# Five kinds of stores issued from GpSimd's queue instead of SP's, in a one-core decoder step

## The chip, the cores and the metric

The kernel runs on one core of one Trainium2 chip. The metric is the device time of one execution in microseconds (us), the median of several runs; lower is better. Engines are named as in the profile: PE (TensorE: matmuls, with its weight loads as PEld), DVE (VectorE), ACT (ScalarE), POOL (GpSimd) and SP (SyncE, which computes nothing here and only issues DMAs). A DMA can be issued from the instruction stream of SP, ACT or POOL. An engine works through its stream in order: a DMA that must wait for its data holds up whatever stands behind it in the same stream.

## The reference

One layer of a hybrid decoder for a prompt of 1024 tokens and 8 sample tokens that share all weights. With d = 1024:

```python
sc_b, sc_c, sc_x, z, xbc, dt_raw, q, gates = jnp.split(xn @ w_in, splits, axis=-1)
conv_u = causal_conv(sc_c * sc_x, width 3)
y_a = (sc_b * conv_u) @ w_sc_out                       # branch A: gated short convolution
...
y_ssd, ssm_new = ssd_fn(xs, dt, a, bm, cm, ssm_s0)     # branch B: 32 heads x 64, state 128
y_ssd = (y_ssd + ssm_d * xs) * silu(z)
y_b = group_rmsnorm(y_ssd, ssm_norm_w, 4) @ w_ssm_out
...
y_c = softmax(q @ mem_k) @ mem_v @ w_attn_o            # branch C: 4 heads x 256, 256 memory tokens
merged = g_a * y_a + g_b * y_b + g_c * y_c             # g = sigmoid(gates)
x = x + merged @ w_merge_o
x = x + swiglu(rmsnorm(x))                             # hidden size 2816
```

The prompt's scan runs in 8 chunks of 128 tokens. Each sample token has its own recurrent state (8 samples x 32 heads x 64 x 128), which is updated once: s = s * exp(dt * a) + (dt * x) * B, and y = s . C. The updated states are outputs, too.

## The kernel before

The kernel is written with a tile framework: it writes instructions in program order, and the framework orders them on the engines, places tiles in a fixed number of buffers per tag, and inserts the semaphore waits. Prompt and sample tokens stand side by side as 1032 columns. Every float32 matmul is done as three: weights and activations are split into a high part (ACT copy) and a rest (DVE subtraction), lines 152 and 153. Raw weights are loaded by SP into a tag with three buffers (line 53, load_raw at line 121), so a raw load has to wait until the DVE has read the raw block three loads earlier.

The stages that the diff touches:

- **Scan stage** (about 540 to 1300 us of the span). PE works on projections of w_in as filler: first the short convolution (sc_step, lines 603 to 634: three projections for each of 8 column blocks, and at the end of the third the DVE's multiplication at line 631 and the store of the result to the scratch array sc_d), then the queries, then the gates. Within each gemm, at three marks, one piece of the scan of branch B is put in (tick, line 168). The scan goes over 4 groups of 8 heads (lines 1173 to 1191), one after another, and for each group over 8 chunks. A chunk c has three pieces (lines 901 to 931): p1 (transposes of x into xp, the products bp/cbm, xdt on the DVE, xdd on POOL; the load r of the decay rows for chunk c + 2, a broadcast of ac_d; s_read for sample c - 2), p2 (matmul pss of chunk c - 1, the state's sum on the DVE, POOL's decay of the state, s_step for sample c - 1, ACT's exponentials of r for chunk c + 1, s_load for sample c + 1) and p3 (matmuls po and py, output yt). r, st and raw weights have three buffers each.
- **Sample states**, inside those pieces: s_load (line 866) loads a state block st of 128 partitions x 512 elements, s_step (line 873) updates it on POOL with lines 879 and 882, and s_read (line 884) stores it to the output and reads it out on the DVE. Of the group's pieces p1 of chunk c holds s_read(c - 2), a round after s_step.
- **End of a group**: z_pieces multiply by silu(z), and group_norm (line 973) ends with four multiplications on the DVE (line 980), each followed by a store of its tile xg[t] to yb_d. The x tiles of the next group are loaded (line 1183) into buffers of the same tags, the third and fourth of them into buffers which these stores read.
- **Attention and output stage** (about 1300 to 1690 us). Filler on PE: the output projections (out_part, line 1420). For every block m a gate tile gt is loaded, multiplied with the matmul's result, added to an earlier partial sum from mg_d in the second and third round, and stored to mg_d. out_in (line 1413) loads the activations of a round. In the pieces run the prompt's attention and, on the side, the samples': s_scores loads key blocks kc into two buffers, s_out (line 1291) does eight samples, and for each stores four rows of 256 elements to os_d; s_back (line 1310) reads os_d back.

Before the change SP issues nearly all loads and these stores; ACT issues stores of its own results (queries, gates, convolved x, attention outputs). POOL issues no DMA at all. In the scan stage POOL runs xdd (776), decay (828), the two lines of s_step and small copies and memsets; in the attention and output stage it runs nothing.

Of the kernel before, what the change touches and what calls it, by code (L numbers as in the profile page):

```python
# [21 lines left out]
TT = T + NS  # L22
# [19 lines left out]
def tile_kernel(ctx: ExitStack, tc, a, o):  # L42
    nc = tc.nc
    V, S, G, PE, SY = nc.vector, nc.scalar, nc.gpsimd, nc.tensor, nc.sync
# [4 lines left out]
    def bc(ap, shape):  # L49
        return ap.to_broadcast(shape)  # L50
# [13 lines left out]
    def sm_ps(name):  # L64
        return psm.tile([P, 512], F32, tag="sm", name=name)

    def dram(name, shape):
        return dp.tile(shape, F32, tag=name, name=name)
# [4 lines left out]
    def flat(ps):  # L73
        return ps[:, :, :CW]

    def t3(t, lo=0):
        return t[:, lo : lo + TT].rearrange("p (n c) -> p n c", n=NCH)
# [78 lines left out]
    def ev_tile(name, shape=(P, TT + 4), dt=F32):  # L156
        return ev.tile(list(shape), dt, tag="ev", name=name)
# [40 lines left out]
    def wblock(w, col):  # L198
        return w[:, col : col + P].rearrange("(k p) c -> p k c", p=P)
# [133 lines left out]
    sc_d = dram("sc_d", [8, P, TT])  # L333
    yb_d = dram("yb_d", [16, P, TT])
    at_d = dram("at_d", [8, P, TT])
    gt_d = dram("gt_d", [24, P, TT])
    mg_d = dram("mg_d", [KD, P, TT])
# [12 lines left out]
    os_d = dram("os_d", [NS, D])  # L350
# [18 lines left out]
    with tc.tile_pool(name="p0", bufs=1) as p0:  # L369
# [13 lines left out]
        for key, src, n in (  # L383
# [14 lines left out]
            while done < n:  # L398
                b, off = divmod(at, P)
                m = min(n - done, P - off)  # L400
# [8 lines left out]
        def par(key, i):  # L409
            return prm[:, PC[key] + i : PC[key] + i + 1]  # L410
# [3 lines left out]
        st = p0.tile([P, 9], F32, tag="st", name="st")  # L414
# [54 lines left out]
    for src, dst, nr, nt in (  # L469
# [4 lines left out]
        for q0 in range(0, nt, per):  # L474
            t = ev_tile(f"hist{nr}_{q0}", (nr, per * P))
# [107 lines left out]
    def proj(col, name):  # L583
        return gemm(weights(wblock(w_in, col), "w" + name), xn, "ps_" + name)

    def conv(acc, u, hist, key, ct, nt, taps, bias):

        w = [par(key, j * nt + ct) for j in range(taps)]
        hv = hist[:, ct, :].rearrange("p (b j) -> p b j", j=taps - 1)
        ap_s = acc[:, T:TT]  # L590
        if bias is None:
            S.activation(acc[:, :T], u[:, 0:T], AF.Copy, scale=w[0])
            V.tensor_scalar(ap_s, hv[:, :, 0], w[0], None, op0=ALU.mult)
        else:
            S.activation(acc[:, :T], u[:, 0:T], AF.Identity, scale=w[0], bias=bias)  # L595
            V.tensor_scalar(ap_s, hv[:, :, 0], w[0], bias, op0=ALU.mult, op1=ALU.add)
        for j in range(1, taps - 1):
            V.scalar_tensor_tensor(acc[:, :T], u[:, j : j + T], w[j], acc[:, :T], op0=ALU.mult, op1=ALU.add)  # L598
            V.scalar_tensor_tensor(ap_s, hv[:, :, j], w[j], ap_s, op0=ALU.mult, op1=ALU.add)
        j = taps - 1  # L600
        V.scalar_tensor_tensor(acc[:, :TT], u[:, j : j + TT], w[j], acc[:, :TT], op0=ALU.mult, op1=ALU.add)

    def sc_step(ct):
        def c_():
            ps = proj(C_SCC + ct * P, f"scc{ct}")
            t = ev_tile(f"csb{ct}")
            S.copy(t3(t), flat(ps))
            return t

        hold = {}  # L610

        def s0():
            hold["c"] = c_()

        def at(col, nm, f):
            return Step(wblock(w_in, col + ct * P), f"w{nm}{ct}", f)

        def s1():
            ps = proj(C_SCX + ct * P, f"scx{ct}")
            u = ev_tile(f"u{ct}")  # L620
            G.memset(u[:, 0:2], 0.0)
            V.tensor_mul(t3(u, 2), flat(ps), t3(hold["c"]))
            G.tensor_copy(tail_sc[:, 0, :, ct], u[:, T : T + 10])
            acc = ev_tile(f"sacc{ct}")
            conv(acc, u, h_sc, "scw", ct, 8, 3, None)
            hold["a"] = acc

        def s2():
            ps = proj(C_SCB + ct * P, f"scb{ct}")
            acc = hold["a"]  # L630
            V.tensor_mul(t3(acc), flat(ps), t3(acc))
            SY.dma_start(sc_d[ct], acc[:, :TT])

        return [at(C_SCC, "scc", s0), at(C_SCX, "scx", s1), at(C_SCB, "scb", s2)]

    def q_step(i):
# [77 lines left out]
    def sp_tile(shape, tag, name, bufs=2):  # L714
        return pool["ssd"].tile(shape, F32, tag=tag, bufs=bufs, name=name)
# [10 lines left out]
    def ssd_pieces(g, xg, bcg):  # L726
# [134 lines left out]
        def s_rows(t, b):  # L861
            return t[0, b, hs].rearrange("h p n -> (h p) n").rearrange("(t q) n -> q t n", q=P)
# [10 lines left out]
        def s_step(b):  # L873
            st, bcb = samp[b]
            xb = sp_tile([P, 4, P], "xb", f"xb{g}_{b}", 1)
            V.tensor_tensor(  # L876
                xb, bc(bcb[:, 0:1, :], [P, 4, P]), bc(hold["xd"][:, :, b : b + 1], [P, 4, P]), op=ALU.mult
            )
            G.tensor_tensor(  # L879
                st, st, bc(es[:, g * 4 : g * 4 + 4, b : b + 1], [P, 4, P]), op=ALU.mult  # L880
            )
            G.tensor_tensor(st, st, xb, op=ALU.add)  # L882

        def s_read(b):
            st, bcb = samp.pop(b)
            SY.dma_start(s_rows(o["s_ssm"], b), st)
            xb = sp_tile([P, 4, P], "xb", f"xc{g}_{b}", 1)
            V.tensor_tensor(xb, bc(bcb[:, 1:2, :], [P, 4, P]), st, op=ALU.mult)
            V.tensor_reduce(hold["ys"][:, :, b : b + 1], xb, axis=AX.X, op=ALU.add)
# [71 lines left out]
    def norm_chunk(sqa, i, n, r, v, name):  # L961

        c = slice(i * CW, (i + 1) * CW)
        ps = sm_ps(f"psn{name}{i}")
        PE.matmul(ps[:, :CW], ones, sqa[:, c], start=True, stop=True)
        V.tensor_scalar(v[:, c], ps[:, :CW], 1.0 / n, EPS, op0=ALU.mult, op1=ALU.add)
        S.activation(sqa[:, c], v[:, c], AF.Sqrt)
        V.reciprocal(r[:, c], sqa[:, c])
        V.tensor_mul(sqa[:, c], r[:, c], r[:, c])
        V.scalar_tensor_tensor(sqa[:, c], v[:, c], -0.5, sqa[:, c], op0=ALU.mult, op1=ALU.mult)  # L970
        V.scalar_tensor_tensor(r[:, c], sqa[:, c], 1.5, r[:, c], op0=ALU.add, op1=ALU.mult)

    def group_norm(g, xg, hold):
        def piece(i):
            if i == 0:
                hold["r"], hold["v"] = ev_tile(f"nr{g}"), ev_tile(f"nv{g}")
            norm_chunk(hold["q"], i, 512, hold["r"], hold["v"], f"y{g}")
            if i == NCH - 1:
                for t in range(4):
                    V.scalar_tensor_tensor(  # L980
                        xg[t], xg[t], par("ssn", g * 4 + t), hold["r"][:, :TT], op0=ALU.mult, op1=ALU.mult
                    )
                    SY.dma_start(yb_d[g * 4 + t], xg[t])

        return [lambda i=i: piece(i) for i in range(NCH)]

# [186 lines left out]
    for g in range(GROUPS):  # L1173
        xg, bcg, hold = [], [], {}
# [44 lines left out]
    if True:  # L1219
# [71 lines left out]
        def s_out(b):  # L1291
            ps = sm_ps(f"pso{b}")
            vcs = []
            for m in range(2):
                vc = at.tile([P, D], F32, tag="kc", name=f"vc{b}{m}")
                SY.dma_start(vc, a["cache_mem_v"][0, b, m * P : (m + 1) * P].rearrange("m h d -> m (h d)"))
                vcs.append(vc)
            for m in range(2):
                for h in range(AH):
                    PE.matmul(  # L1300
                        ps[32 * h : 32 * h + 32, :256], pTs[:, m, :], vcs[m][:, h * 256 : (h + 1) * 256],
                        start=(m == 0), stop=(m == 1),
                    )
            t = at.tile([P, 256], F32, tag="so", bufs=1, name=f"so{b}")
            S.copy(t, ps[:, :256])
            for h in range(AH):
                row = 32 * h + b * AH + h
                SY.dma_start(os_d[b : b + 1, h * 256 : (h + 1) * 256], t[row : row + 1, :])

        def s_back():  # L1310
            t = ev_tile("osr", (NS, D))
# [94 lines left out]
        for b in range(NS):  # L1406
            pieces += [lambda b=b: s_out(b), None]
# [12 lines left out]
        def out_part(w, m, gate, more, nm):  # L1420
            gt = ev_tile(f"gt{nm}")
            SY.dma_start(gt[:, :TT], gt_d[gate])
            ps = gemm(weights(wblock(w, m * P), f"wo{nm}"), acts, f"po{nm}")
            V.tensor_mul(t3(gt), flat(ps), t3(gt))  # L1424
            if more:
                t = ev_tile(f"mg{nm}")
                SY.dma_start(t[:, :TT], mg_d[m])
                V.tensor_add(gt[:, :TT], gt[:, :TT], t[:, :TT])
            SY.dma_start(mg_d[m], gt[:, :TT])

        for i, (src, w) in enumerate(
            ((sc_d, a["w_sc_out"][0]), (yb_d, a["w_ssm_out"][0, 0:D]), (yb_d[8:16], a["w_ssm_out"][0, D : 2 * D]))
# [25 lines left out]
    for m in range(KD):  # L1458
        merged.append(big(f"mg{m}"))
        SY.dma_start(merged[m], mg_d[m])  # L1460
        gt = ev_tile(f"gt3{m}")
# [60 lines left out]
    for half in range(2):  # L1522
        sq = ev_tile(f"sq{half}")
        for m in range(KD):
# [16 lines left out]
            t = x2[m][:, HS[half]]  # L1541
# [139 lines left out]
    st = fin.tile([P, 18], F32, tag="fst", name="fst")  # L1681
# [76 lines left out]
```

## Time and profile before

| | |
|---|---|
| median of 3 runs | 2601.65 us (2600.45 to 2602.65) |
| profiled execution, own time | 2603.75 us |
| its span (first to last instruction) | 2601.7 us |
| mean granted TensorE clock | 0.988 |
| POOL busy | 197.9 us, 211 instructions |
| DMAs on SP's queue (q1) | 335.74 MB |
| DMAs on ACT's queue (q10) | 50.84 MB |

The profile is of one execution. Its rows have an engine, a line (L976 is line 976), what is written and read by the program's names, a count and durations. In a timeline row the bracket at the end is the idle time of the engine just before, and what ended it. A row of the waits says who waited for whom, then us in total, times, and the longest. "SPq" is SP issuing a DMA: its duration is that of the issue, not of the transfer. The chain is the path followed back from the last instruction, at each step to what released it.

### The profile page before, as it was taken

The numbers are of one execution on the slowest core, as the hardware profiler recorded it, in microseconds if no ns is written. First come the engines' busy times: TensorE is split into PE (matmuls) and PEld (weight loads), VectorE is DVE, ScalarE is ACT, GpSimd is POOL, SyncE is SP. The second block draws the span as 40 slices with busy tenths as digits, with TensorE's granted clock in tenths as the row PEclk, the third lists the DMA queues.
The fourth block names the chain that finished last, engine by engine and source line by source line (L and its number), as shares of the span: only waits on it lengthen the run. The fifth ranks groups of instructions, "written<-read, shape, count | busy, mean of one in ns | idle before, by whom it ended". The sixth has DMA issues, their size and how long they took to land.

```text
span 2601.7 us, 42760 instructions
## 1 busy us (share of the span) xinstructions
PE 2521.7 (97%) x18037; PEld 2453.8 (94%) x18037; DVE 1466.5 (56%) x2037; ACT 936.6 (36%) x1434; POOL 197.9 (8%) x211
## 2 busy tenths in 40 slices
PE   7999999999998999999999999999989999999998
PEld 5899999999998999999999898999979999999998
DVE  5844586866667655555566633444784445454316
ACT  6643444553232235354342322213343333341202
POOL 0000000013213123023000000000010000000000
PEclk9999999999999999999999999999989999999999
DMA  6244333376556755665487757854322222265211
GB/s 190 94 138 156 124 104 106 123 206 148 154 157 138 161 185 160 176 196 150 133 292 243 273 175 252 299 173 144 122 73 82 74 90 66 82 212 163 66 41 66
DMA packets 391422, 389.31 MB, mean 150 GB/s; under 512 B 15622, under 2 KB 337782, under 8 KB 391223
## 3 DMA queue, kind: packets, MB, share of 16 engines
q1 hardware_dynamic: 372654, 335.74, 43.4%
q10 hardware_dynamic: 18577, 50.84, 5.1%
q8 instruction: 142, 2.33, 0.4%
q14 instruction: 49, 0.40, 0.0%
HBM read 280.41 MB, written 106.34 MB: 149 GB/s over the span
## 4 chain that ended last, share of the span: by engine, by line
PE 68%; DMA 5%; DVE 4%; issue 1%; ACT 1%; SPq 0%; POOL 0%; ACTq 0%; DVEq 0%; POOLq 0%
PE ps_g L192 10%; PE po L192 10%; PE pd L192 8%; PE ps_scc L192 4%; PE pm L1535 4%; PE ps_q L192 4%; PE ps_scx L192 3%; PE ps_scb L192 3%; DMA kc<-in_cache_mem_k_dram 1%; PE py L797 1%; PE pss L815 1%; PE po L789 1%; DMA r<-ac_d 1%; PE u20m L236 1%; PE g20m L236 1%
## 5 line engine op out<-in xcount | busy, mean ns | idle before, releaser
L1658 DVE TENSOR_TENSOR x<-pd,x 128x1032 f32<-128x1032 f32 x24 | 29.5, 1231 | 131.4 <-PE pd L192 131.4
L742 ACT ACTIVATE r<-r,acum 128x128 f32<-128x128 f32 x256 | 78.9, 391 | 36.2 <-DMA r<-ac_d 34.8
L1424 DVE TENSOR_TENSOR gt<-po,gt 128x1032 f32<-128x1032 f32 x24 | 29.5, 1230 | 70.4 <-PE po L192 69.1
L776 POOL TENSOR_TENSOR xdd<-xdt,decst 128x512 f32<-128x512 f32 x32 | 46.6, 1456 | 268.1 <-DVE xdt L772 268.1
L1583 POOL TENSOR_TENSOR x<-x,x 128x516 f32<-128x516 f32 x4 | 8.9, 2235 | 635.8 <-DVE x L1502 635.8
L598 DVE SCALAR_TENSOR_TENSOR ax<-u,prm,ax 128x1024 f32<-128x1024 f32 x44 | 56.4, 1281 | 0.3 <-ACT ax L595 0.3
L882 POOL TENSOR_TENSOR st<-st,xb 128x512 f32<-128x512 f32 x32 | 43.8, 1368 | 36.2 <-DVE xb L876 34.0
L769 ACT COPY bT<-bp 128x128 f32<-128x128 f32 x32 | 8.5, 264 | 105.4 <-DVE cbm L767 105.4
L770 DVE TENSOR_TENSOR r<-r,cbm 128x1024 f32<-128x1024 f32 x32 | 39.1, 1222 | 8.6 <-ACT r L743 8.0
L806 DVE SCALAR_TENSOR_TENSOR x<-x,dpar,yt 128x128 f32<-128x128 f32 x128 | 37.5, 354 | 10.1 <-ACT yt L804 9.2
L828 POOL TENSOR_TENSOR s<-s,cdec 128x512 f32<-128x512 f32 x28 | 39.1, 1398 | 46.1 <-DVE s L821 29.6
L821 DVE TENSOR_TENSOR s<-pss,s 128x512 f32<-128x512 f32 x28 | 19.3, 688 | 38.8 <-PE pss L815 38.8
L815 PE MATMUL pss<-xdd,bT 128*128 128x512 f32 x64 | 33.8, 610 | 6.6 <-ACT bT L769 6.5
L879 POOL TENSOR_TENSOR st<-st,es 128x512 f32<-128x512 f32 x32 | 36.6, 1143 | 20.3 <-DMA st<-in_state_ssm_dram 16.7
L797 PE MATMUL py<-r,xdt 128*64 128x128 f32 x512 | 35.0, 279 | 1.5 <-issue 1.5
L767 DVE TENSOR_TENSOR cbm<-bp,tri 128x128 f32<-128x128 f32 x32 | 9.3, 290 | 45.3 <-PE bp L762 45.2
L743 ACT ACTIVATE r<-r 128x1024 f32<-128x1024 f32 x32 | 33.9, 1059 | 0.7
L793 DVE TENSOR_TENSOR yt<-po,ea 128x512 f32<-128x512 f32 x28 | 19.2, 686 | 25.7 <-PE po L789 25.7
L797 PEld LDWEIGHTS py<-r,xdt 128*64 128x64 f32 x512 | 27.3, 136 | 5.8 <-issue 2.4
L1263 ACT ACTIVATE pr<-psa,mx 128x256 f32<-128x256 f32 x32 | 14.9, 472 | 48.8 <-DVE mx L1261 48.8
L1253 DVE TENSOR_TENSOR kc<-kc,qb 128x1024 f32<-128x1024 f32 x16 | 19.6, 1224 | 22.0 <-DMA kc<-in_cache_mem_k_dram 21.9
L1542 DVE TENSOR_TENSOR x<-pm,xT 128x516 f32<-128x516 f32 x16 | 11.1, 695 | 36.2 <-PE pm L1535 36.2
(7961 smaller groups left out, 8684.3 us busy)
## 6 DMA issues: line engine op xcount, KB each, us to landing
gt<-gt_d SPq DMA_DIRECT2D x32, 516.0 KB
r<-ac_d SPq DMA_DIRECT2D x32, 512.0 KB
gt_d<-g ACTq DMA_DIRECT2D x24, 516.0 KB
mg_d<-gt SPq DMA_DIRECT2D x24, 516.0 KB
mg<-mg_d SPq DMA_DIRECT2D x24, 516.0 KB
xs_d<-ax ACTq DMA_DIRECT2D x22, 516.0 KB
hr<-h_d SPq DMA_DIRECT2D x22, 516.0 KB
zs_d<-z ACTq DMA_DIRECT2D x16, 516.0 KB
```

What stands on the lines that cost most here:

```text
L192: PE.matmul(ps[:, n, :CW], wt[:, ks], x[:, n * CW : (n + 1) * CW], start=(k == 0 and i == 0), stop=(k == nk - 1 and i == 2),)
L236: PE.matmul(ps[:, n, :HC], wt[:, ks], x[:, n * HC : (n + 1) * HC], start=(start and kt == 0 and i == 0), stop=(kt == 3 and i == 2), skip_g ...
L598: V.scalar_tensor_tensor(acc[:, :T], u[:, j : j + T], w[j], acc[:, :T], op0=ALU.mult, op1=ALU.add)
L742: S.activation(r[:, h, :], r[:, h, :], AF.Relu, scale=-1.0, bias=acum[:, c, h0 + h : h0 + h + 1])
L770: V.tensor_tensor(r, r, bc(cbm.unsqueeze(1), [P, HPG, P]), op=ALU.mult)
L776: G.tensor_tensor(b3(xdd, HPG), b3(xdt, HPG), bc(decst[:, c, hs].unsqueeze(2), [P, HPG, 64]), op=ALU.mult)
L797: PE.matmul(py[hp : hp + 64, (h // 2) * P : (h // 2 + 1) * P], xdt[:, h * 64 : (h + 1) * 64], r[:, h, :], start=True, stop=True,)
L806: V.scalar_tensor_tensor(xg[t][:, cs], xg[t][:, cs], dpar[:, g * 4 + t : g * 4 + t + 1], yt[:, t, :], op0=ALU.mult, op1=ALU.add,)
L815: PE.matmul(pss, bT, xdd, start=True, stop=True)
L828: ins = G.tensor_tensor(b3(s_new, HPG), b3(state["s"], HPG), bc(cdec[:, c, hs].unsqueeze(2), [P, HPG, 64]), op=ALU.mult,)
L882: G.tensor_tensor(st, st, xb, op=ALU.add)
L1535: PE.matmul(ps[:, n, :HC], wt[:, ks], x[:, half * HT + n * HC : half * HT + (n + 1) * HC], start=(k == 0 and i == 0), stop=(k == KD - 1 an ...
```

## The change

Five `dma_start` calls go from SP (`SY`) to POOL (`G`). Four stay at their place in the source: the short convolution's result (8 stores of 516 KB), the normed scan output (16 of 516 KB), the rows of the samples' attention output (32 of 1 KB) and the partial sums (24 of 516 KB). The fifth, the store of the sample states (32 of 256 KB), also moves: from the start of s_read to the end of s_step, right behind POOL's addition. All loads stay on SP.

```diff
@@ sc_step
             V.tensor_mul(t3(acc), flat(ps), t3(acc))
-            SY.dma_start(sc_d[ct], acc[:, :TT])
+            G.dma_start(sc_d[ct], acc[:, :TT])
@@ s_step
             G.tensor_tensor(st, st, xb, op=ALU.add)
+            G.dma_start(s_rows(o["s_ssm"], b), st)
 
         def s_read(b):
             st, bcb = samp.pop(b)
-            SY.dma_start(s_rows(o["s_ssm"], b), st)
             xb = sp_tile([P, 4, P], "xb", f"xc{g}_{b}", 1)
@@ group_norm
-                    SY.dma_start(yb_d[g * 4 + t], xg[t])
+                    G.dma_start(yb_d[g * 4 + t], xg[t])
@@ s_out
-                SY.dma_start(os_d[b : b + 1, h * 256 : (h + 1) * 256], t[row : row + 1, :])
+                G.dma_start(os_d[b : b + 1, h * 256 : (h + 1) * 256], t[row : row + 1, :])
@@ out_part
-            SY.dma_start(mg_d[m], gt[:, :TT])
+            G.dma_start(mg_d[m], gt[:, :TT])
```

## The prediction

> **What bounds the kernel now.** I read the head of the page first, then the busy time by stretches, then the waits of SP's queue, then every idle gap of PE in the stages that the diff touches. In the stretch rows the columns after the sum are PE, PEld, DVE, ACT and POOL, then the granted clock, the DMA share and GB/s.
>
> ```profile
> span 2601.7 us, 42760 instructions
> PE 2521.7 (97%) x18037; PEld 2453.8 (94%) x18037; DVE 1466.5 (56%) x2037; ACT 936.6 (36%) x1434; POOL 197.9 (8%) x211
> 540.00:1300.00 760.00, 747.99 (x4988) 717.52 (x4989) 454.51 (x653) 289.75 (x496) 173.98 (x147) 0.99 0.60 161
> 1300.00:1690.00 390.00, 376.76 (x2438) 358.95 (x2437) 203.10 (x261) 115.12 (x201) 0.00 (x0) 0.99 0.76 255
> 800.00:850.00 50.00, 43.49 (x280) 40.60 (x279) 31.17 (x42) 18.59 (x44) 17.73 (x15) 0.93 0.53 130
> ```
>
> TensorE is busy for 97% of the span. All moved stores lie between 540 and 1690 us (scan stage, then attention and output stage), and there PE is idle for 12.0 and 13.2 us. So a gain can only come out of these few gaps and the slower clock after them. SP's queue, in contrast, waits a great deal, and in large part for the data of the stores:
>
> ```profile
> SPq L886 <- POOL st L882: 166.4, 28, 12.4
> SPq L868 <- DMA out_s_ssm_dram<-st: 38.0, 6, 9.6
> SPq L983 <- DVE x L980: 34.2, 15, 9.0
> SPq L1308 <- ACT so L1305: 30.9, 7, 7.1
> SPq L1429 <- DVE pTl L1361: 26.6, 4, 14.3
> SPq L1429 <- DVE gt L1428: 21.8, 9, 7.1
> ```
>
> The columns are us in total, times, longest. Waits for the data of a store hold SP's queue for some 280 us (166.4 + 34.2 + 30.9 + 26.6 + 21.8). The question is in which of these waits something is late that TensorE needs. PE's gaps of the scan stage that I can tie to a DMA are these three:
>
> ```profile
> 663.21 0.66 PE L765 MATMUL xp<-ident,x 128*128 128x128 f32 x4 [2.25 <-DVE yt L802]
> 844.17 2.04 PE L815 MATMUL pss<-xdd,bT 128*128 128x512 f32 x2 [6.51 <-ACT bT L769]
> 1123.31 0.33 PE L765 MATMUL xp<-ident,x 128*128 128x128 f32 x1 [0.61 <-DMA x<-xs_d]
> ```
>
> The bracket is the idle time and what ended it. A stall costs more than its gap, since the matmuls after it are slow: the chain shows, for the same work, quick and slow rows.
>
> ```profile
> 669.52 0.86 PE pss L815 x2
> 674.61 2.83 PE ps_scc L192 x18
> 844.17 2.04 PE pss L815 x2
> 846.21 3.98 PE ps_scc L192 x18
> 663.87 5.65 PE ps_scb L192 x26
> 670.38 4.23 PE ps_scb L192 x27
> ```
>
> So the stall at 844 costs 6.51 + 1.18 + 1.15 = 8.84 us. At 663 the 26 matmuls took 5.65 us where 26/27 of 4.23 = 4.07 were due: 2.25 + 1.58 = 3.8 us.
>
> **What goes: 112 stores leave SP's queue.** Whether that shortens the 8.84 us is the main term. The chain into the gap runs through a store of sample states. Here are SP's issues, then the DVE instruction that matters:
>
> ```profile
> 785.40 0.45 SPq L124 DMA_DIRECT2D wscx7r<-in_w_in_dram  x1
> 799.55 0.46 SPq L124 DMA_DIRECT2D wscb7r<-in_w_in_dram  x1
> 821.15 0.43 SPq L868 DMA_DIRECT2D st<-in_state_ssm_dram  x1
> 830.24 0.38 SPq L886 DMA_DIRECT2D out_s_ssm_dram<-st  x1
> 830.72 0.45 SPq L124 DMA_DIRECT2D wq1r<-in_w_in_dram  x1
> 831.22 11.59 DMA r<-ac_d
> 826.99 2.07 DVE L153 TENSOR_TENSOR wscx7l<-wscx7r,wscx7h 128x1024 fp32r<-128x1024 f32 x1
> 641.03 1.23 DVE L153 TENSOR_TENSOR wscc3l<-wscc3r,wscc3h 128x1024 fp32r<-128x1024 f32 x1 [2.62 <-ACT wscc3h L152]
> 642.29 0.37 SPq L124 DMA_DIRECT2D wscc4r<-in_w_in_dram  x1
> ```
>
> SP has nothing to issue from 821.6 to 830.24, where the store's data is done. The decay rows (r) that stall ACT, and behind it bT and PE, are loaded only at 831.22. At first sight the whole 8.6 us is the store's. But between store and r stands the weight load wq1r. Raw weights have three buffers (line 53), and the three raw loads before wq1r are wscx7r, wscb7r and wq0r. So wq1r takes the buffer of wscx7r, which the DVE reads until 826.99 + 2.07 = 829.06. Without the store in the queue, wq1r would wait there until 829.06, and r would follow at about 829.6 instead of 831.2. **Another wait takes its place: the gain is 1.6 us, not 8.8.** The stall at 663 shows the same with the store out of the way: its r load comes behind wscc4r, issued at 642.29, just when the DVE ends with wscc3l (641.03 + 1.23 = 642.26), whose buffer wscc4r takes. There I count no gain.
>
> In the attention stage the queue's long waits hold the key loads only in appearance:
>
> ```profile
> SPq L1252 <- DVE sc_s L1254: 22.0, 8, 6.0
> SPq L1417 <- DMA mg_d<-gt: 8.5, 4, 3.4
> ```
>
> A key load (L1252) waits for its own two buffers, and the loads of out_in (L1417) wait until a partial-sum store has landed, since it frees an ev buffer. Both waits stay. Before the loads from at_d SP waits for the last partial sum, and that goes; I set it against the later landing of the stores and count the stage at nothing.
>
> **What is added: the stores on POOL.** No row shows a DMA issued by POOL, so its price has to be bounded.
>
> ```profile
> L983 SPq DMA_DIRECT2D yb_d<-x x16: 319/329/339, 732.4 to 1297.1; - x16
> L868 SPq DMA_DIRECT2D st<-in_state_ssm_dram x32: 368/428/4244, 547.9 to 1211.9; - x32
> L776 POOL TENSOR_TENSOR xdd<-xdt,decst 128x512 f32<-128x512 f32 x32 | 46.6, 1456 | 268.1 <-DVE xdt L772 268.1
> L1308 SPq DMA_DIRECT2D os_d<-so x32: 237/246/636, 1558.7 to 1635.7; - x32
> ```
>
> The three numbers are shortest/median/longest in ns. From below: what SP needs for the same store, 0.33 us; on a ring of its own, not behind SP's loads, a store could even land sooner than now. From above: the longest single issue in these rows, 4.24 us. I take POOL's own ordinary instruction, 1.46 us (nearest in engine), for one issue. So a store reaches the DMA engines later by d = 1.46 - 0.33 = 1.13 us, with bounds of below 0 and 3.9 us.
>
> For POOL itself that is nothing. It waits 268 us in 32 times before xdd alone, 8.4 us a chunk, and its product xdd of one chunk is used by the matmul only in the next piece round (first(c) writes it, third(c) runs in p2(c + 1)). The state store also moves in the source, from s_read to s_step, and now stands behind the addition L882 on the same engine, for whose end it waits. It delays xdd, decay and the small copies, and has this cover of 8.4 us; a longer issue would show as pss waiting for xdd. sc_d waits on POOL for the multiplication of line 631; xdd comes behind it, but its input xdt stands later in the DVE's own order. The four os_d stores of a sample need 4 x 1.46 = 5.8 us of the 11.0 us (77.0 us over 7) between samples. mg_d has POOL to itself. A state store that lands later by d lengthens SP's six waits of L868 for its buffer; that load is for a step two piece rounds on, which hides 1 us.
>
> Where it is not nothing is behind yb_d. At the start of groups 1 to 3 the third and fourth x tile of the next group go into buffers that the store frees on landing:
>
> ```profile
> 1111.77 4.63 DMA yb_d<-x
> 1116.41 6.85 DMA x<-xs_d
> 936.01 0.17 DVE L857 TENSOR_TENSOR xds<-x,dts 128x8 f32<-128x8 f32 x1 [1.18 <-DMA x<-xs_d]
> 936.08 0.60 PE L765 MATMUL xp<-ident,x 128*128 128x128 f32 x4
> ```
>
> For group 3 the chain ends in PE's gap of 0.61 us: slack zero. For group 2 the tile lands at 936.01 and PE takes it at 936.08: slack 0.07. For group 1 I found no wait of PE or DVE for x, so the slack is unknown and I take zero. Taking SP's wait away doesn't help, as the x loads (L1183) then wait for the same landing. So a later store is paid in full at three places: 3 x 1.13 - 0.07 = 3.3 us. Gaps as short as that I count without slow matmuls.
>
> **Sum.** -1.6 + 3.3 = +1.7 us. The profiled execution took 2603.75 us for a span of 2601.7; the median of the runs shown is 2601.65. I add the difference to the median: 2603.4 us. What a measurement here can tell from no change is about 0.2%, 5.2 us, so this forecast is "the same".
>
> One rule speaks against the whole idea. The Trainium skill, "DMA: Bandwidth & Descriptors", section "Issuing engines are not separate DMA queues", says that DMAs from any engine end on the same 16 DMA engines, and more issuing engines save only issue time. By that alone the sum would be 0, and 2601.65. The page's section "SWDGE vs HWDGE vs iDMA" adds that POOL's descriptors are computed in software; its table of first-byte latency (about 1 us against 0.6) gives, as an estimate, d = 0.4 and a sum of -0.5 us.
>
> **The rivals.**
>
> *The order changes in favour of r.* In the source, load(c + 2) stands ahead of s_read and of the next weights. If the queue without stores issues r ahead of the weight load, or the weights' buffer comes free earlier, both stalls go: -8.84 - 3.8 + 3.3 = -9.3, 2592.3 us. For it: r's own buffer is free in time (only 13.2 us of waits of L736 for py in the whole stage, row below). Against it: nothing in the diff touches that order.
>
> ```profile
> SPq L736 <- PE py L797: 13.2, 5, 5.7
> ```
>
> *The stores land much later (the other side).* Place: yb_d at the three group starts. Once d is over 2.25 us each gap is as long as the one at 663, which drew 1.58 us of slow matmuls. With d = 3.1, half way from there to the upper bound: -1.6 + 9.2 + 3 x 1.6 = +12.4, 2614 us; at the upper bound 3.9 it is 2616.5. It decides from d = 2.25, where the gaps alone give -1.6 + 6.7 = +5.1. For it: four stores come one after another, each 1.2 us behind the last, on an engine that needs 1.0 to 1.5 us for everything. Against it: the second and later ones hardly matter if POOL keeps pace.
>
> *Only issue time moves (the skill's rule).* r comes as late as now because DMA, not the queue, is slow (11.59 us for one load), and a store lands as now because the ring costs nothing: 0, 2601.65 us.
>
> **How the numbers follow.** Forecast (the wait changes its name, d about 1): 0.38, between 2600 and 2608. Order in favour of r: 0.22. Stores land much later: 0.28. Only issue time: 0.12. Faster by over 0.2%: 0.22 + 0.02 of the forecast = 0.24. Slower: 0.28 + 0.06 of it = 0.34. Within: 0.30 + 0.12 = 0.42. The range reaches from the one rival to the other, 2592 to 2615, and leaves out about a tenth on each side.
>
> **What would show it.** Right: the SP wait for st (L886) is gone, but the waits of L124 for the DVE's L153 grow in the scan stage; the gap at 844 shrinks by under 2 us; the chain at the group starts still has yb_d, then x, and xp waits about 1 us more; a POOL issue takes about 1.5 us. Wrong: r issued ahead of the weights and no gap at 844 (first rival); POOL issues over 2.6 us, or yb_d landing over 2 us later (second); xdd or decay ending a wait of PE; and a queue order that differs elsewhere, which I can't derive from the diff.

## The result and the profile after

The changed kernel takes 2622.74 us (2618.25 to 2627.11), the kernel before 2601.05 us in the same runs: a ratio of 1.0081, 95% interval [1.0068, 1.0094]. By this ratio it is 21 us slower; forecast was +1.7 us with an upper bound of 2615.

The head of the page after, SP's waits that are longest among the loads of the scan stage, and the busy time by stretches (us, then the sum, PE, PEld, DVE, ACT and POOL, clock, DMA share, GB/s):

```profile
span 2619.5 us, 42844 instructions
PE 2527.6 (96%) x18037; PEld 2459.2 (94%) x18037; DVE 1464.0 (56%) x2037; ACT 936.0 (36%) x1434; POOL 264.1 (10%) x323
```
```profile
SPq L870 <- DVE xc L888: 63.7, 21, 5.9
SPq L868 <- DMA out_s_ssm_dram<-st: 62.9, 12, 11.1
SPq L736 <- PE py L797: 43.6, 7, 9.6
SPq L752 <- DVE yt L793: 42.8, 12, 8.1
```
```profile
540.00:1300.00 760.00, 746.81 (x4985) 716.49 (x4986) 453.66 (x653) 289.49 (x496) 211.91 (x203) 0.99 0.59 161
1300.00:1690.00 390.00, 367.90 (x2373) 350.69 (x2371) 191.64 (x252) 106.87 (x193) 27.82 (x55) 0.99 0.75 253
```

SP no longer waits for the data of a store; it waits for free buffers instead (L868 62.9 us where it was 38.0, L736 43.6 where it was 13.2). In the scan stage PE is idle for 13.2 us where it was 12.0 (760 less the PE column), in the attention and output stage for 22.1 us where it was 13.2. Most is lost in the attention and output stage, which the prediction counted "at nothing".

The scan stage hides a gain and a loss. These are PE's three gaps there, to be held against the three of before (2.25, 6.51 and 0.61 us):

```profile
662.10 0.66 PE L765 MATMUL xp<-ident,x 128*128 128x128 f32 x4 [2.01 <-DVE yt L802]
838.21 1.71 PE L815 MATMUL pss<-xdd,bT 128*128 128x512 f32 x2 [3.20 <-ACT bT L769]
1118.98 0.47 PE L765 MATMUL xp<-ident,x 128*128 128x128 f32 x1 [6.50 <-DMA x<-xs_d]
```

The forecast gap has halved, and a new one of 6.50 us stands at the start of group 3. To see where time is won and lost along the whole kernel, I took from the PE timelines the first matmul of a weight block and subtracted the time of the same block in the kernel before (us; the other rows are runs that follow):

```
kernel               wscc3  wscc7    wg9   wg10   wo20   wo24   wo30   wo32
after                -2.65  -6.30  -5.91  +0.54  +2.38 +11.89  +9.82 +17.96
a1_ssm               -1.68  -4.94  -5.22  -5.09  -3.26  -3.27  -3.76  -4.00
a2_yb                -0.55  -1.28  -0.80  +5.65  +7.75  +7.75  +7.25  +7.11
a4_mg                -0.91  -1.08  -1.25  -1.15  -0.50  +6.28  +4.21 +12.63
b1_mg_pinned         +0.25  -0.35  -0.68  -0.24  +1.24  +1.40  +0.93  +2.24
b2_mg_order_alone    -2.25  -2.70  -3.06  -2.77  -2.54  +4.74  +2.67 +11.72
b4_all_pinned        -1.75  -5.84  -5.86  -5.69  -2.84  -2.85  -3.30  -1.33
```

The numbers in the names count weight blocks; the columns stand in order of time. A column alone holds the spread of two executions, so the steps between columns are what counts. A step has a spread too: b1_mg_pinned loses 1.9 us from wg9 to wo20, where it differs from the kernel before in a few partial-sum stores alone. The changed kernel wins 3.7 us at the 844 stall (wscc3 to wscc7), loses 6.5 at the start of group 3 (wg9 to wg10), 9.5 among the samples' attention products (wo20 to wo24) and 8.1 at the start of the at_d round (wo30 to wo32).

At these three places the two built programs differ in a way that the diff doesn't show: **the framework has put other instructions in another order**. Even with the moved stores left out of the comparison, PE's stream differs at each of them, and the streams of the DVE, ACT and SP differ, too. That gave the two theories for the runs. **Theory 1, order:** the time is lost because engines and queues run in another order. **Theory 2, late landing:** a store issued by POOL lands later and frees its buffer later (the prediction's second rival, with the output stage added).

### The profile page after: what moved, and what is told of

It is laid out like the page before. It is cut to its first block, busy times and chain, and to the rows that moved or that the text cites. A ratio compares the mean times of both kernels' runs of the same rounds, so it can differ in the third digit from the quotient of the medians.

```text
span 2619.5 us, 42844 instructions
## 1 busy us (share of the span) xinstructions
PE 2527.6 (96%) x18037; PEld 2459.2 (94%) x18037; DVE 1464.0 (56%) x2037; ACT 936.0 (36%) x1434; POOL 264.1 (10%) x323
## 4 chain that ended last, share of the span: by engine, by line
PE 64%; DMA 8%; DVE 4%; issue 2%; ACT 1%; SPq 0%; POOL 0%; ACTq 0%; DVEq 0%; POOLq 0%
PE ps_g L192 10%; PE pd L192 8%; PE po L192 6%; PE ps_scc L192 4%; PE pm L1535 4%; PE ps_scx L192 3%; PE ps_q L192 3%; PE ps_scb L192 3%; DMA kc<-in_cache_mem_k_dram 2%; PE py L797 1%; PE pss L815 1%; DMA mg_d<-gt 1%; DMA in<-yb_d 1%; PE po L789 1%; DMA in<-at_d 1%
## 5 line engine op out<-in xcount | busy, mean ns | idle before, releaser
L1424 DVE TENSOR_TENSOR gt<-po,gt 128x1032 f32<-128x1032 f32 x24 | 29.5, 1228 | 91.7 <-PE po L192 91.6
L1429 POOL DMA_DIRECT2D mg_d<-gt x24 | 13.0, 541 | 339.1 <-DVE gt L1428 177.3
L1464 DVE TENSOR_TENSOR gt<-po,gt 128x1032 f32<-128x1032 f32 x8 | 9.9, 1232 | 42.2 <-PE po L192 42.2
```

## The experiments

| run | on POOL | order | us | before, us | ratio, 95% interval |
|---|---|---|---|---|---|
| a1_ssm | state stores | its own | 2598.44 | 2601.31 | 0.9990 [0.9982, 0.9999] |
| a2_yb | normed output | its own | 2610.01 | 2601.31 | 1.0032 [1.0020, 1.0044] |
| a3_os | sample rows | its own | 2601.93 | 2601.31 | 1.0006 [0.9997, 1.0014] |
| a4_mg | partial sums | its own | 2614.48 | 2601.31 | 1.0054 [1.0041, 1.0067] |
| b1_mg_pinned | partial sums | of before | 2604.51 | 2600.51 | 1.0011 [1.0002, 1.0020] |
| b2_mg_order_alone | none | of a4_mg | 2615.45 | 2600.51 | 1.0060 [1.0047, 1.0073] |
| b3_yb_pinned | normed output | of before | 2601.51 | 2600.51 | 1.0004 [0.9995, 1.0012] |
| b4_all_pinned | all five | of before | 2601.97 | 2600.51 | 1.0006 [0.9997, 1.0015] |
| c1_mg_pe_pinned | partial sums | PE: of before | 2620.87 | 2601.48 | 1.0077 [1.0064, 1.0090] |
| c2_mg_sp_pinned | partial sums | SP: of before | 2609.65 | 2601.48 | 1.0037 [1.0026, 1.0049] |
| c3_three_pinned | states, short conv, sample rows | of before | 2599.26 | 2601.48 | 0.9989 [0.9981, 0.9997] |
| c4_yb_order_alone | none | of a2_yb | 2608.07 | 2601.48 | 1.0036 [1.0023, 1.0050] |

### One kind of store at a time

Each kernel is the one before with one of the diff's parts. For a1_ssm:

```diff
             G.tensor_tensor(st, st, xb, op=ALU.add)
+            G.dma_start(s_rows(o["s_ssm"], b), st)
         def s_read(b):
             st, bcb = samp.pop(b)
-            SY.dma_start(s_rows(o["s_ssm"], b), st)
```

> Only the 32 stores of sample states go to POOL, at the place they have in the changed kernel. Theory 1 (order): the loss comes from instructions that the framework puts in another order, and this store changes the order of no engine but SP's loads, so only the gain remains: the gaps at 663 and 844 us shrink as in the changed kernel (-2.7 and -3.7 us by its trace), -5 to -7 us in all. Theory 2 (late landing): each store issued by POOL lands about 1 us later and frees its buffer later; the next state load waits, but two piece rounds hide it: the same gain, -4 to -6 us. What was forecast before the result (another wait takes the place): -1.6 us.

> Only the 16 stores of the normed scan output go to POOL. Theory 1 (order): at the starts of groups 2 and 3 the x loads now stand behind the store and loads of the sample rows (bc_d, bcb) on SP, so at the start of group 3 PE waits about 6 us for x as in the changed kernel (6.50 us against 0.61), +6 to +8 us in all, and little at groups 1 and 2. Theory 2 (late landing): three group starts pay about 1 to 2 us each for a store that lands later, +3 to +6 us, with the yb_d transfer itself longer than the 4.63 us of before.

> Only the 32 stores of one sample row of 1 KB (os_d) go to POOL; 32 KB in all. Theory 1 (order): the framework puts the samples' attention products and the loads of the output stage in another order when these waits leave SP; the 8 to 9 us between blocks wo20 and wo23 of the changed kernel come back here, and part of the 8 us at the start of the at_d round: +6 to +15 us. Theory 2 (late landing of large stores): such small stores fill no queue and free one small buffer; at most +2 us.

> Only the 24 stores of partial sums go to POOL. Theory 1 (order): the order of the output stage changes here too (PE, DVE and ACT run it otherwise than before), about the 8 us at the start of the at_d round and some of the 8 to 9 us between wo20 and wo23: +8 to +17 us. Theory 2 (late landing): the store lands 6.3 us after its issue instead of some 5.3, ev buffers come free 1 us later in 24 places of which few are critical, and the last one ahead of the at_d round costs most: +3 to +8 us, at the start of the at_d round alone.

Measured were -0.10%, +0.32%, +0.06% and +0.54%. The four add up to +0.82%, and the whole change gives +0.81%: within the intervals the parts add up (the short-convolution stores were not run alone). a1_ssm gained 2.9 us by the medians, less than either theory expected; the 3.3 us at the 844 stall are there, but in the table above some 2 us are gone again between wg10 and wo20; why isn't shown, and b1_mg_pinned loses 1.5 us there, too. a3_os is a miss for theory 1: the order of the output stage changes there as much as in a4_mg (about 200 lines of difference in PE's stream in each), and it costs next to nothing. So a changed order is not a loss by itself; it depends on what then stands in front of what. a4_mg (+13.2 us by the medians) came out as theory 1 had it; a2_yb (+8.7) lies just above theory 1's range, which ends at 8, and not far above theory 2's, which ends at 6. The next runs hold order and queue apart.

### The order held, the queue changed, and the reverse

The framework takes order edges between instructions of one engine; they add no wait. ORDER lists the instructions of PE, ACT, DVE and SP as they stand in a reference program, without the moved stores, and each is tied to the one ahead of it, in the stages that the texts below name:

```diff
-        tile_kernel(tc, ins, outs)
+        tile_kernel(tc, ins, outs); pin(tc)
+def pin(tc):
...
+    for runs in ORDER:
...
+                if last is not None:
+                    tc.add_manual_dep(ins, last.name, info, reason="pin")
+                last = ins
```

> The partial sums go to POOL as in a4_mg (+13.2 us), but every instruction of PE, ACT, DVE and SP in the attention and output stage is tied to the order that it has in the kernel before (order edges alone, no waits). Theory 1 (order): the loss goes with the order, so -2 to +3 us against before. Theory 2 (late landing): the stores still land later and free their ev buffers later, so most of the loss stays: +8 to +13 us.

> The reverse: all stores stay on SP, but PE, ACT, DVE and SP's loads are tied to the order that they have in a4_mg; the framework puts the partial-sum stores among SP's loads. Theory 1 (order): +8 to +15 us, with PE's waits for vc among the samples' products and for b01h at the start of the at_d round. Theory 2 (late landing): the stores land as before, so within 3 us of before, though SP's waits for their data stand in a queue in which more loads are ahead.

> The normed scan output goes to POOL as in a2_yb (+8.7 us), with every instruction of PE, ACT, DVE and SP of the scan stage tied to the order of before, so that the x loads stand ahead of bc_d and bcb again. Theory 1 (order): the gap of 6 us at the start of group 3 is gone, -2 to +2 us. Theory 2 (late landing): the x loads still wait for a later landing at three group starts, +4 to +9 us.

> All five kinds of stores on POOL, as in the changed kernel (+21.7 us), with PE, ACT, DVE and SP's loads tied to the order of before from the scan stage to the end of the output stage. Theory 1 (order): the loss is gone and the gain of the state stores (a1_ssm: -2.9 us) stays: -6 to 0 us against before. Theory 2 (late landing): the state stores' gain, and a large part of the loss of the normed output and the partial sums: +8 to +20 us.

> All stores stay on SP; PE, ACT, DVE and SP's loads are tied to the order that they have in a2_yb, in which bc_d and bcb stand ahead of the x loads at the start of groups 2 and 3. Theory 1 (order): the gap of PE at the start of group 3 is there without any store on POOL, +5 to +9 us. Theory 2 (late landing): within 2 us of before.

In the built programs the instructions of PE, ACT and DVE and SP's other DMAs stand in b1, b3 and b4 exactly as in the kernel before, in b2 as in a4_mg and in c4 as in a2_yb. So this decides it for these two kinds of store, in which the loss lies. With the stores on POOL and the old order, the normed output costs nothing that can be measured (1.0004), the partial sums 0.1%, and all five together 0.06%, an interval that holds 1. With the stores left on SP and the new order, the loss is there without any store on POOL: 1.0060 where a4_mg had 1.0054, 1.0036 where a2_yb had 1.0032. **The order makes the loss; the queue makes at most 0.2% for the partial sums (b1's interval).** Of theory 2 a small part remains: b1 is above 1, and by the medians (+4.0 us) above the 3 us at which theory 1's range ends. b4 loses 2 us from wo30 to wo32, which c3_three_pinned (below), with the partial sums on SP, does not lose, and came out above the upper end of theory 1 (+1.5 us by the medians, expected -6 to 0). Its 1.0006 is a net: c3_three_pinned, which has the normed output and the partial sums back on SP, has 0.9989, so these two cost about 0.17% on POOL even in the old order, near the sum of b3 and b1 (0.15%). The order of the whole change was not run with all stores on SP, nor the kernel before tied to its own order; what the edges themselves cost is bounded only by b3 and b4, whose intervals hold 1.

**How an order costs time: group 3.** PE's timeline in the kernel before (start, us, then the instruction, and in brackets the idle time before it):

```profile
1118.01 0.38 PE L765 MATMUL xp<-ident,x 128*128 128x128 f32 x2
1118.15 0.72 PE L192 MATMUL ps_g<-xnh,wg9h 128*128 128x344 f32 x3
...
1120.13 0.32 PE L192 MATMUL ps_g<-xnl,wg9h 128*128 128x344 f32 x1
1120.96 0.33 PE L765 MATMUL xp<-ident,x 128*128 128x128 f32 x1 [0.51 <-DMA x<-xs_d]
```

and in c4_yb_order_alone, where no store has left SP, with SP's queue and the chain behind it:

```profile
1115.38 0.38 PE L765 MATMUL xp<-ident,x 128*128 128x128 f32 x2
1122.05 0.47 PE L765 MATMUL xp<-ident,x 128*128 128x128 f32 x1 [6.29 <-DMA x<-xs_d]
1122.17 1.21 PE L192 MATMUL ps_g<-xnh,wg9h 128*128 128x344 f32 x3
1123.18 1.06 PE L192 MATMUL ps_g<-xnl,wg9h 128*128 128x344 f32 x3
```
```profile
1107.93 3.93 SPq L983 DMA_DIRECT2D yb_d<-x  x4
1111.95 0.31 SPq L724 DMA_DIRECT2D bc_d<-bcr  x1
1114.80 0.93 SPq L870 DMA_DIRECT2D bcb<-bc_d  x2
1115.78 1.14 SPq L1183 DMA_DIRECT2D x<-xs_d  x2
```
```profile
1111.95 2.83 DMA bc_d<-bcr
...
1115.78 6.22 DMA x<-xs_d
```

In the old order PE fills the wait for the third x tile with matmuls of a gate (1118.15 to 1120.45) and stands idle for 0.51 us. In the new order the third transpose stands right behind the second, and PE can't pass it: 6.29 us idle, and the next three matmuls take 1.21 us, where the three at 1118.15 of before took 0.72. On SP, the x loads stand behind the bcb loads, and these wait for bc_d to land. b3_yb_pinned has the old order with the stores on POOL, and its gap is short again:

```profile
1122.52 0.33 PE L765 MATMUL xp<-ident,x 128*128 128x128 f32 x1 [1.41 <-DMA x<-xs_d]
```

What later landing costs there can't be told from this gap. b1_mg_pinned has the old order and its yb_d stores on SP, and a longer gap at the same place:

```profile
1123.07 0.33 PE L765 MATMUL xp<-ident,x 128*128 128x128 f32 x1 [1.77 <-DMA x<-xs_d]
```

In all kernels with yb_d on SP and PE's old order here, PE's waits for x at this place add up to between 0.66 (a3_os) and 1.98 us (c2_mg_sp_pinned); on POOL they are 1.41 (b3) and 1.50 (b4). The store whose landing this chain waits for took 4.95 (b3) and 4.96 us (b4) from its issue to landing on POOL, and 4.56 to 5.33 us in the eight kernels whose chain shows it on SP. In the built program of a2_yb, the third and fourth transposes are the only PE instructions that stand elsewhere than before.

**The output stage.** SP's queue in the kernel before, then in a4_mg, then PE there:

```profile
1566.13 0.33 SPq L1296 DMA_DIRECT2D vc<-in_cache_mem_v_dram  x1
...
1569.40 3.05 SPq L1417 DMA_DIRECT2D in<-yb_d  x3
1572.50 4.04 SPq L1296 DMA_DIRECT2D vc<-in_cache_mem_v_dram  x2
```
```profile
1571.65 5.98 SPq L1417 DMA_DIRECT2D in<-yb_d  x3
1577.68 0.43 SPq L1296 DMA_DIRECT2D vc<-in_cache_mem_v_dram  x1
1578.66 2.60 SPq L1417 DMA_DIRECT2D in<-yb_d  x2
...
1582.50 1.03 SPq L1296 DMA_DIRECT2D vc<-in_cache_mem_v_dram  x2
```
```profile
1582.49 0.64 PE L1300 MATMUL pso<-vc,pTs 128*32 128x256 f32 x8 [2.97 <-DMA vc<-in_cache_mem_v_dram]
1590.55 0.64 PE L1300 MATMUL pso<-vc,pTs 128*32 128x256 f32 x8 [1.25 <-DMA vc<-in_cache_mem_v_dram]
```

In the old order a value block vc goes ahead of the three loads of out_in (1566.13) and two more follow them; in the new order one block follows the three (1577.68), and the two more stand behind two further loads (1582.50). These loads wait for ev buffers, and PE meets the samples' products before vc is there (2.97 and 1.25 us). At the start of the at_d round the DVE's order differs. Before:

```profile
1676.14 1.23 DVE L163 TENSOR_TENSOR b01l<-in,b01h 128x1032 fp32r<-128x1032 f32 x1 [2.60 <-ACT b01h L162]
1677.34 1.23 DVE L1424 TENSOR_TENSOR gt<-po,gt 128x1032 f32<-128x1032 f32 x1
1678.48 1.23 DVE L163 TENSOR_TENSOR b02l<-in,b02h 128x1032 fp32r<-128x1032 f32 x1
```

and in a4_mg, with SP's loads and ACT ahead of it:

```profile
1673.74 8.38 SPq L1417 DMA_DIRECT2D in<-at_d  x3
1684.79 1.05 ACT L162 CAST b01h<-in 128x1032 fp32r<-128x1032 f32 x1 [8.47 <-DMA in<-at_d]
1685.87 1.24 DVE L163 TENSOR_TENSOR b01l<-in,b01h 128x1032 fp32r<-128x1032 f32 x1 [8.29 <-ACT b01h L162]
1687.15 1.24 DVE L163 TENSOR_TENSOR b02l<-in,b02h 128x1032 fp32r<-128x1032 f32 x1
1688.30 1.23 DVE L1424 TENSOR_TENSOR gt<-po,gt 128x1032 f32<-128x1032 f32 x1
```

The product gt of the last partial sum (L1424) now stands behind b02l, and the DVE first waits 8.29 us for an activation of the next round. So the last partial sum is late, and with it a load: SP waits 0.7 us for its addition (L1428), which frees a buffer, before it can issue another load of at_d. But the activation is late, too: SP issues its load at 1673.74, the first of the three, and ACT has it at 1684.79, 11.1 us later, where it was 6.2 us before (1668.89 to 1675.05). No run changes the DVE's order alone, so how the loss here is split between the DVE's order and the loads isn't shown.

### Which engine's order

> Partial sums on POOL, only PE tied to its order of before; DVE, ACT and SP stay as the framework orders them. If the samples' attention products that PE takes too early cause the loss between wo20 and wo23 (6.8 us in a4_mg), that part goes and the 8.4 us at the start of the at_d round stay, for they come from the loads and the DVE: +6 to +10 us in all. If PE's order causes all of it: 0 to +3 us. If it is the loads that PE waits for in any order: +12 to +15 us.

> Partial sums on POOL, only SP's loads tied to their order of before; PE, DVE and ACT stay as the framework orders them. If SP's order causes the loss at the start of the at_d round (weights of that round ahead of its activations), the 8.4 us there go and the part between wo20 and wo23 stays: +5 to +9 us. If PE's and DVE's order causes both: +11 to +15 us. If SP's order causes both: 0 to +3 us.

c1 (+19.4 us by the medians) lies above all three of its ranges; c2 (+8.2) lies in the first of its ranges, but of the 8.4 us that were to go there most stays. With PE alone in the old order the kernel is, if anything, slower than with none (+0.77% against +0.54%, the intervals overlap a little): PE now comes to the first of the samples' products while SP still loads in the new order, and waits longer for vc.

```profile
1582.76 1.08 PE L1300 MATMUL pso<-vc,pTs 128*32 128x256 f32 x8 [6.38 <-DMA vc<-in_cache_mem_v_dram]
1693.53 1.23 PE L192 MATMUL po<-b01h,wo30h 128*128 128x344 f32 x3 [3.61 <-ACT b01h L162]
```

With SP alone in the old order 0.37% are left, and the start of the at_d round still loses 5.5 us of the 8.4 (wo30 to wo32 in its timeline; its profiled execution, 2616.06 us, is the longest of its six, whose median is 2609.65). Neither PE's order nor SP's alone takes the loss away. But the framework also placed the untied engines anew: in the built programs their order in c1 and c2 is not that of a4_mg. So these runs don't isolate an engine; that the orders of the engines and of SP's queue have to fit each other is argued, not shown. I did not split it further.

### The version that the runs point to

> State stores, short-convolution results and sample rows on POOL, normed output and partial sums on SP, with the order of before on all other engines: the version that the runs so far point to. Theory 1 (order): -3 to -6 us, a little better than a1_ssm (-2.9 us), as the 2 us that b4_all_pinned lost at the start of the at_d round and 1.8 us at wo01 belong to stores that are now on SP. Theory 2 (late landing): the state stores' gain alone, -1 to -3 us.

0.9989, 2.2 us by the medians: faster than both kernels by a little, and no better than a1_ssm, which is one line moved and needs no order edges. By theory 1 I had hoped for 3 to 6. About 0.1% is the most that any version run here gained.

## Why the prediction was wrong

**The 844 stall: mechanism right, the gain half of what it was.** I wrote that another wait takes the place of the store's: wq1r would wait for the DVE's wscx7l, "and r would follow at about 829.6 instead of 831.2". The profile after shows just that, first on the DVE, then on SP and in the chain:

```profile
824.33 2.07 DVE L153 TENSOR_TENSOR wscx7l<-wscx7r,wscx7h 128x1024 fp32r<-128x1024 f32 x1
826.46 0.37 SPq L124 DMA_DIRECT2D wq1r<-in_w_in_dram  x1
826.92 0.53 SPq L736 DMA_DIRECT2D r<-ac_d  x1
```
```profile
826.92 9.92 DMA r<-ac_d
```

SP's wait for st (L886) is gone, and its waits of L124 for the DVE's L153 in the scan stage grew from some 154 to 269 us, as forecast. The first rival, r ahead of the weights, did not come about: wq1r still goes first.

PE stands 2.65 us earlier here than before (the table), so 831.22 would be 828.57: r is issued 1.65 us earlier, 1.6 was forecast. But the load then took 9.92 us instead of 11.59, 1.67 us less, and 1.65 + 1.67 are the 3.31 us by which the gap shrank. I had kept a transfer's time fixed while its start moved. The shorter load is no accident of one execution: it took 9.67 to 10.17 us in the four kernels with the state stores on POOL, and 10.71 to 11.59 us in the ten with them on SP, so the 11.59 of before is at the long end. Why it is shorter stays open. The DMA share between 800 and 850 us does not tell: it is 0.48 in a1_ssm, where the load took 10.17 us, and 0.48 in a4_mg, where it took 11.42.

**The 663 stall: right.** I counted no gain. The changed kernel's PE does win 1.8 us at this place against the profiled execution of before. But so does that of a4_mg, which touches nothing in the scan stage (1.6 us), and of c4_yb_order_alone, which has no store on POOL (2.2 us); so it is the spread of one execution, not the change.

**The price of POOL: too high.** I took 1.46 us for an issue and d = 1.13. POOL's issues are far shorter:

```profile
L883 POOL DMA_DIRECT2D out_s_ssm_dram<-st x32: 767/793/956, 580.1 to 1247.1; - x32
L983 POOL DMA_DIRECT2D yb_d<-x x16: 532/534/550, 730.1 to 1298.0; - x16
L1429 POOL DMA_DIRECT2D mg_d<-gt x24: 531/534/567, 1347.8 to 1697.5; - x24
L1308 POOL DMA_DIRECT2D os_d<-so x32: 484/484/505, 1562.3 to 1634.0; - x32
```

For yb_d that is 0.2 us more than SP's 0.33, and the 4.95 us from issue to landing at the start of group 3 lie inside the 4.56 to 5.33 that SP's stores took there, so that no d can be told from zero. The term of 3.3 us at three group starts is too large as well: with the order held, b3_yb_pinned measured +1.0 us by the medians, an interval that holds 0. The rival "the stores land much later" decided from d = 2.25 and is refuted, though the time came out on its side. POOL's own work was hidden, as forecast: no wait of PE ends with POOL in the stages of the change.

**The step that failed** is a sentence under the first rival, "nothing in the diff touches that order", and with it the output stage counted at nothing. I worked out each queue as the old one with the stores taken out. The framework makes the order anew for all engines, and in that order PE takes transposes and products while their loads are still under way, and the DVE takes next round's activations ahead of this round's last sum. The runs put a price on it: the order alone, with every store on SP, costs 0.60% (that of a4_mg) and 0.36% (that of a2_yb); the same stores on POOL in the old order cost 0.11% and 0.04%. I had named "a queue order that differs elsewhere, which I can't derive from the diff" among what would make the prediction wrong, and gave it no price and no chance. The profile of before could have shown one place where it can bite: PE waits only 1.1 us for x at the start of group 3, because matmuls of a gate stand between the transposes. At vc and b01h PE does not wait at all before; that filler is the reason there is argued, not shown.

**The rival "only issue time moves".** With the order held, the sum of all five moves is 1.0006 [0.9997, 1.0015]. The Trainium skill, "DMA: Bandwidth & Descriptors", section "Issuing engines are not separate DMA queues", says that more issuing engines save only issue time. b4_all_pinned agrees with it in sum, though its 1.0006 is the net of a gain at the 844 stall and a small cost of the other stores. By itself the rule does not tell what an order made anew will cost; the whole change, order and queue together, cost 0.8% here.

## What to carry to other kernels

In a kernel whose order is made by a framework, a moved instruction is not the only thing that moves: compare the built programs engine by engine before reasoning about queues, and where a loss appears, tie the old order to the new queue and the new order to the old queue, since the two runs split the cost. Look for PE instructions whose load is covered by filler standing ahead of them, as the transposes of group 3 were; a new order can expose them. When a store's wait leaves a queue, look for the next wait behind it, here a weight buffer: of the 8.6 us between SP's last issue and the store's, r came only 1.65 us earlier.

## What the runs showed of the hardware

- A DMA issued by POOL held it for 0.53 us at 516 KB, 0.79 us at 256 KB in the state's form (128 partitions x 4 x 128), and 0.48 us for a single row of 1 KB; the row costs almost as much there as the large store.
- From issue to landing, a yb_d store of 516 KB at the start of group 3 took 4.95 (b3) and 4.96 us (b4) on POOL, and 4.56 to 5.33 us in eight kernels with it on SP.
- The same 512 KB broadcast load (r, at the 844 stall) took 9.67 to 10.17 us in four kernels with the state stores on POOL, and 10.71 to 11.59 us in the ten with them on SP. The cause is open.
